# A hybrid attention and state-space layer: every float32r tile at multiples of 64 bytes, a set order around the first LayerNorm and the first FFN block, and LayerNorm's scale in the transposes' eviction

## The chip, the cores and the metric

The kernel runs on one core of a Trainium2 chip. Its time is the device time of one execution, in microseconds (us). Before the change the median of three runs is 1178.77 us (1176.41 to 1178.85).

## The reference

One decoder layer for 512 tokens of width 1024, all in float32. A combined projection gives the queries, keys, values and forget gates of an attention part, the z, x, B, C and dt of a Mamba-2 part, and two branch gates. Both branches are projected to 1024 columns, merged by the gates and projected once more. Two LayerNorms and a SwiGLU FFN with 2816 hidden columns follow:

```
proj = x @ w_in
q, k, v, f_logit, z, xbc, dt_raw, gate_logit = split(proj)
attn_d = forgetting_attention(q, k, v, log_sigmoid(f_logit + b_forget)) @ w_proj_attn
ssm_d  = mamba2_branch(z, xbc, dt_raw, ...) @ w_proj_ssm
gates  = sigmoid(gate_logit + b_gates)
mixed  = (gates[0] * attn_d + gates[1] * ssm_d) @ w_out
x = layer_norm(alpha * x + mixed, ln1_g, ln1_b)
h = (silu(x @ w_ffn_gate) * (x @ w_ffn_up)) @ w_ffn_down
x = layer_norm(alpha * x + h, ln2_g, ln2_b)
```

## The kernel before

**Products.** Each float32 GEMM is three matmuls of float32r operands (`mm3`, L113 to L116). Both operands are split (L79 to L81): `hi` is a cast on ScalarE (ACT), `lo` the rest, a subtraction on VectorE (DVE). The three are hi times hi, hi times lo and lo times hi. TensorE holds 128x128 of the one operand (stationary, the second name in a profile row) and streams the columns of the other (moving, the first name), 512 or 256 at a time. Weights come from DRAM in tiles of 128x1024 (`raw`), 512 KB a load on SyncE's queue (SP), and are split under high priority into `whi` and `wlo` (three buffers each).

**Order of the work.** Projections with the scan, in four groups; attention; the branch gates and the merge (up to 757 us); the output projection; the first LayerNorm; six column blocks of the FFN; the down projection with the second LayerNorm. A scheduler puts each engine's instructions in an order; where nothing has priority that is nearly the order of the code.

**The output projection** (`gemm_down`, L151) runs in four quarters: two pairs of 128-token tiles (`th_`) by two column halves, 48 matmuls of 512 columns each. `evac_res` (L684 to L687) adds the residual and takes the statistics of a half row. `layer_norm` (L689 to L699) joins them into `mv`, takes the root on GpSimd (POOL, L693), and applies mean, gain, root and bias in two DVE instructions of 1024 columns, with gain and bias spread over all partitions in `t_gz`. The result goes to DRAM as `x1_d` (L728), and in 16 transposes for each token pair (L733) to PSUM. From there ACT copies it to `xf` (L739), and for tokens 0 and 1 a split makes the FFN operands B11 and B21 (L738).

**The FFN** computes each GEMM of 512 hidden columns (256 in the last block) with seven products of quarters, in this order of passes: P1, P2, P6, P5, P7, P3, P4. A pass is 24 matmuls of 256 columns (12 in the last block). The token operands are B11, B21, NT2, NT1, T3, B22 and T4 (`x_operands`, made all at once). The weight operands are quarters or sums of quarters: a11, a12, a11 + s1, s1, s3, a12 + a11, a22. s1 and s3 are sums of two quarters, made by a load on SP and an adding load on POOL (L787, L789); the other sums are DVE's (L807, L812). Their splits stand under high priority (L792 to L798). A block b has a gate GEMM (Gb in this text, PSUM banks `gps`) and an up GEMM (Ub, banks `cps`). Banks are emptied by a copy, a sum, and SwiGLU's two steps (L830, L833, L877 to L881). Block 0 runs two passes of G0 and of U0, then the operands, then the rest.

**The down projection** takes `h`, split again, against 22 weight chunks of 24 matmuls of 512 columns, 528 in all. The residual comes back from `x1_d` (L915), and the second LayerNorm stands at the end.

**Places in SBUF.** Pools place tiles one behind another, from the left or right end. In the programs as built the float32r operands begin at these bytes, modulo 128:

| | before | after |
| --- | --- | --- |
| xh, xl, t_uh, t_ul, t_xtok, t_gz, t_bT, t_cT, t_btok, t_cbm, t_xst, t_xdt, t_v, t_th | 64 | 64 |
| whi, wlo (stream of weights), t_ab, t_nw, t_hn | 96 | 64 |
| FFN tokens b11, b21 | 96 | 64 |
| FFN tokens nt1, nt2, t3, t4, b22, down projection ht | 32 | 64 |
| FFN weights wh, wl: two of the four buffers / the other two | 96 / 32 | 64 / 64 |

Of the kernel before, what the change touches and what calls it, by code (L numbers as in the profile page):

```python
# [37 lines left out]
def tile_hybrid_decoder_layer(  # L38
# [681 lines left out]
    xop = {"B11": operand(bop, "b11"), "B21": operand(bop, "b21")}  # L720
    for th_ in range(2):
        tts = (2 * th_, 2 * th_ + 1)
        for half in ((1, 0), (0, 1))[th_]:
            gemm_down(wo_chunk, KD, tok(mx), tts, half, evac_res, gps)
        for tt in tts:
            for _ in layer_norm(tt, gb):
                pass
            nc.gpsimd.dma_start(out=x1_d[tt], in_=xr[tt])  # L728
            for i in range(2):
                ps = cps()  # L730
                for k in range(4):
                    kt = 4 * i + k
                    nc.tensor.transpose(out=ps[:, k * P:(k + 1) * P], in_=xr[tt][:, kt * P:(kt + 1) * P], identity=ident)  # L733
                ps = ps.rearrange("p (k t) -> p k t", k=4)
                ts = slice(tt * P, (tt + 1) * P)
                if th_ == 0:
                    hi, lo = xop[("B11", "B21")[i]]
                    split(hi[:, :, ts], lo[:, :, ts], ps)  # L738
                nc.scalar.copy(out=xf[i][:, :, ts], in_=ps)  # L739

    left1.close()
    hb = pool(ctx, "hb", "left")
    tp = pool(ctx, "tp", "left")
    top = pool(left2, "top", "left")
    wops.append(pool(left2, "wop1", "left"))
    nops = [0]
    tmp2 = pool(left2, "tmp2", "left")

    def t_tile(dtype=F32):
        return tp.tile([P, 1024], dtype, name="T", bufs=4)

    def x_operands():
        B = {(k, t): xf[k - 1][:, :, (t - 1) * 256:t * 256] for k in (1, 2) for t in (1, 2)}

        def new(nm, make):
            t = t_tile().rearrange("p (k t) -> p k t", k=4)
            make(t)
            xop[nm] = operand(top, nm.lower())  # L760
            split(*xop[nm], t)
            return t
        v = nc.vector
        nt1 = t_tile().rearrange("p (k t) -> p k t", k=4)
        v.tensor_tensor(out=nt1, in0=B[1, 1], in1=B[1, 2], op=ALU.subtract)
        nt2 = new("NT2", lambda t: v.scalar_tensor_tensor(out=t, in0=nt1, scalar=-1.0, in1=B[2, 2], op0=ALU.mult, op1=ALU.subtract))
        xop["NT1"] = operand(top, "nt1")
        split(*xop["NT1"], nt1)
        new("T3", lambda t: v.tensor_tensor(out=t, in0=B[2, 2], in1=B[1, 2], op=ALU.subtract))
        xop["B22"] = operand(top, "b22")  # L770
        split(*xop["B22"], B[2, 2])
        new("T4", lambda t: v.scalar_tensor_tensor(out=t, in0=nt2, scalar=-1.0, in1=B[2, 1], op0=ALU.mult, op1=ALU.subtract))
# [44 lines left out]
    PASSES = (("X", "B11"), ("Y", "B21"), ("X", "NT2"), ("Z", "NT1"), ("X", "T3"), ("Z", "B22"), ("X", "T4"))

    def ffn_gemm(w, c0, F, alloc, quadrant):


        nj = F // P
        n = nj * 256
        ops = quarters(w, c0, F)
        bank = {}
        cp = {}

        def keep(nm, src):
            cp[nm] = tmp2.tile([P, T], F32, name="cp", bufs=4)[:, 0:n]
            nc.scalar.copy(out=cp[nm], in_=src)  # L830

        def add(nm, src):
            nc.vector.tensor_tensor(out=cp[nm], in0=src, in1=cp[nm], op=ALU.add)  # L833
            return cp[nm]

        for i, (b, x_) in enumerate(PASSES):
# [128 lines left out]
```

## Time and profile before

| | us |
| --- | --- |
| median of three runs | 1178.77 (1176.41 to 1178.85) |
| profiled execution | 1178.42 |
| its span | 1176.7 |
| TensorE busy in the span | 1138.1 |
| VectorE busy | 770.5 |
| ScalarE busy | 525.6 |
| GpSimd busy | 135.6 |

The mean granted TensorE clock is 0.988 of full speed. The profile has five engines: PE (matmuls), PEld (PE's weight loads, beside its matmuls), DVE, ACT and POOL, and SP for loads. A row out<-in gives the tile written and the tiles read, "x" a count. For a matmul the names behind the arrow are moving, stationary.

### The profile page before, as it was taken

How to read it: one execution, taken by the hardware profiler on the slowest of the kernel's cores; microseconds unless marked ns; L12 is line 12 of the kernel's file. 1: busy time of each engine (PE TensorE's matmuls, PEld its weight loads, DVE VectorE, ACT ScalarE, POOL GpSimd, SP SyncE). 2: the span in 40 equal slices, each digit the busy share in tenths (PEclk: the TensorE clock that was granted, in tenths of full speed). 3: DMA queues.
4: the chain of work that ended last, by engine and by line, in shares of the span. 5: the costliest groups of instructions: out<-in, count | busy, mean ns of one | idle time of the engine just before them, and what ended most of it. 6: DMA issues, size and time to landing. Idle time of an engine off the chain costs nothing.

```text
span 1176.7 us, 15773 instructions
## 1 busy us (share of the span) xinstructions
PE 1138.1 (97%) x6086; PEld 947.5 (81%) x6086; DVE 770.5 (65%) x1210; ACT 525.6 (45%) x906; POOL 135.6 (12%) x165
## 2 busy tenths in 40 slices
PE   7999999999999999999999999989799999999997
PEld 5787877778777788777777888877799999988885
DVE  3579964883885654887788344556787777764326
ACT  3376773453441423665566353213454544453120
POOL 2003131030231100211110000021001111100001
PEclk8999999999999999999999999989899999999999
DMA  8343243243231233121211355372577877473311
GB/s 241 91 129 125 73 126 90 78 116 95 90 91 55 89 90 93 52 73 55 73 55 55 90 161 161 119 203 79 118 199 176 201 179 171 94 252 97 103 54 72
DMA packets 115707, 134.20 MB, mean 114 GB/s; under 512 B 5588, under 2 KB 93872, under 8 KB 115504
## 3 DMA queue, kind: packets, MB, share of 16 engines
q1 hardware_dynamic: 99328, 112.80, 31.4%
q0 software_dynamic: 14576, 14.09, 7.6%
q10 hardware_dynamic: 1728, 6.29, 1.5%
q8 instruction: 48, 0.79, 0.3%
q14 instruction: 27, 0.22, 0.1%
HBM read 128.77 MB, written 4.26 MB: 113 GB/s over the span
## 4 chain that ended last, share of the span: by engine, by line
PE 45%; DVE 3%; issue 3%; DMA 1%; ACT 1%; POOL 1%; SPq 0%; DVEq 0%; POOLq 0%; ACTq 0%
PE gps L114 9%; PE gps L116 9%; PE gps L115 9%; PE cps L116 5%; PE cps L115 5%; PE cps L114 5%; DMA rq<-in_w_ffn_up_dram 1%; PE cps L433 1%; PE cps L427 1%; DVE xr L698 0%; DVE wl L81 0%; POOL mv L693 0%; PE cps L405 0%; DVE t_sd L698 0%; DMA t_sd<-in_x_dram 0%
## 5 line engine op out<-in xcount | busy, mean ns | idle before, releaser
L81 DVE TENSOR_TENSOR wlo<-raw,whi 128x1024 fp32r<-128x1024 f32 x127 | 156.2, 1230 | 226.5 <-ACT whi L80 226.2
L80 ACT CAST whi<-raw 128x1024 fp32r<-128x1024 f32 x127 | 132.9, 1047 | 279.4 <-PE gps L116 113.1
L114 PE MATMUL gps<-xh,whi 128*128 128x512 f32 x456 | 183.2, 402 | 0.0
L115 PE MATMUL gps<-xl,whi 128*128 128x512 f32 x456 | 183.0, 401 | 0.0
L116 PE MATMUL gps<-xh,wlo 128*128 128x512 f32 x456 | 182.9, 401 | 0.0
L80 ACT CAST wh<-rq 128x1024 fp32r<-128x1024 f32 (+1 forms) x84 | 81.9, 978 | 123.8 <-PE cps L115 46.6
L81 DVE TENSOR_TENSOR wl<-rq,wh 128x1024 fp32r<-128x1024 f32 (+1 forms) x84 | 94.9, 1133 | 42.3 <-ACT wh L80 42.1
L115 PEld LDWEIGHTS gps<-xl,whi 128*128 128x128 f32 x456 | 86.0, 189 | 18.0 <-issue 0.2
L114 PEld LDWEIGHTS gps<-xh,whi 128*128 128x128 f32 x456 | 85.9, 188 | 18.1 <-issue 0.2
L116 PEld LDWEIGHTS gps<-xh,wlo 128*128 128x128 f32 x456 | 86.0, 189 | 17.2
L114 PE MATMUL gps<-whi,xh 128*128 128x512 f32 x192 | 77.4, 404 | 3.8 <-ACT xh L80 3.8
L115 PE MATMUL gps<-wlo,xh 128*128 128x512 f32 x192 | 77.1, 402 | 0.0
L116 PE MATMUL gps<-whi,xl 128*128 128x512 f32 x192 | 77.1, 402 | 0.0
L212 DVE SCALAR_TENSOR_TENSOR t_v<-gps,cw,t_v 128x511 f32<-128x511 f32 (+2 forms) x72 | 53.5, 745 | 4.4 <-ACT t_v L209 3.6
L116 PE MATMUL gps<-t_uh,wlo 128*128 128x512 f32 x128 | 51.7, 404 | 0.0
L115 PE MATMUL gps<-t_ul,whi 128*128 128x512 f32 x128 | 51.6, 403 | 0.0
L114 PE MATMUL gps<-t_uh,whi 128*128 128x512 f32 x128 | 51.2, 400 | 0.0
L114 PEld LDWEIGHTS gps<-whi,xh 128*128 128x128 f32 x192 | 36.6, 191 | 13.6 <-ACT xh L80 4.5
L789 POOL DMA_DIRECT2D rq<-in_w_ffn_gate_dram x12 | 15.5, 1294 | 265.9 <-PE gps L116 168.8
L412 ACT ACTIVATE t_y<-t_y,sm 128x128 f32<-128x128 f32 (+1 forms) x64 | 35.7, 559 | 19.4 <-DVE sm L410 17.7
L115 PEld LDWEIGHTS gps<-wlo,xh 128*128 128x128 f32 x192 | 36.7, 191 | 9.2 <-DVE wlo L81 0.5
L116 PEld LDWEIGHTS gps<-whi,xl 128*128 128x128 f32 x192 | 36.5, 190 | 9.1 <-DVE xl L81 0.3
(562 smaller groups left out, 2782.1 us busy)
## 6 DMA issues: line engine op xcount, KB each, us to landing
raw<-in_w_in_dram SPq DMA_DIRECT2D x80, 512.0 KB, 3.7
rq<-in_w_ffn_gate_dram SPq DMA_DIRECT2D x25, 512.0 KB, 6.1
rq<-in_w_ffn_up_dram SPq DMA_DIRECT2D x25, 512.0 KB, 4.9
raw<-in_w_ffn_down_dram SPq DMA_DIRECT2D x22, 512.0 KB, 3.7
t_ab<-ac_d SPq DMA_DIRECT2D x32, 256.0 KB, 3.4
raw<-in_w_proj_ssm_dram SPq DMA_DIRECT2D x16, 512.0 KB, 3.5
rq<-in_w_ffn_gate_dram POOLq DMA_DIRECT2D x10, 512.0 KB, 6.9
rq<-in_w_ffn_up_dram POOLq DMA_DIRECT2D x10, 512.0 KB, 6.0
```

Of the source, the lines that this page charges most:

```text
L80: nc.scalar.copy(out=hi, in_=src)
L81: nc.vector.tensor_tensor(out=lo, in0=src, in1=hi.bitcast(F32), op=ALU.subtract)
L114: nc.tensor.matmul(out=o, lhsT=l[0], rhs=r[0], start=start, stop=False, skip_group_check=skip)
L115: nc.tensor.matmul(out=o, lhsT=l[0], rhs=r[1], start=False, stop=False, skip_group_check=skip)
L116: nc.tensor.matmul(out=o, lhsT=l[1], rhs=r[0], start=False, stop=stop, skip_group_check=skip)
L212: nc.vector.scalar_tensor_tensor(out=v[:, sh:], in0=ps[:, 0:T - sh], scalar=cw[:, k, blk:blk + 1], in1=v[:, sh:], op0=ALU.mult, op1=ALU.add)
L412: nc.scalar.activation(out=pt[:, 0:n], in_=pt[:, 0:n], func=AF.Exp, scale=-1.0, bias=sm[:, 2:3], accum_out=sm[:, 0:1])
L427: nc.tensor.transpose(out=ps[:, o:o + P], in_=pr[i][:, kb * P:(kb + 1) * P], identity=ident)
L433: nc.tensor.matmul(out=po[:, kb * P:], lhsT=vt[:, kb, hh, :], rhs=pT[kb][j], start=kb == 0 and j == 0, stop=kb == NT - 1 and j == 1)
L789: nc.gpsimd.dma_start(out=v(t), in_=s_, accum_op=ALU.add)
```

## The change

1. **Places.** A tile of 32 bytes a partition ahead of the right pools (`pad`) and one in `hb` (`pad2`); `lnv` takes 64 bytes of `cst0`, and `mv` has two buffers for four. The table above has what follows.
2. **LayerNorm.** The first one only normalises: one DVE instruction of 1024 columns, (x - mean) * root. ln1's gain and bias are loaded as 16 more rows of a transpose at the start (`lnv`), and stand as scale and bias in ACT's eviction of each transpose, 128 columns apiece, in place of one copy of 512. `x1_d` holds the normalised rows; behind the reload before the down projection, eight DVE instructions apply gain and bias to them.
3. **Order.** A class `Gemm` takes the place of the generators: loads, operands, multiply and evacuate are written out for block 0; from there on an operand is made two passes ahead, without priority, and loads stand at fixed passes. `rq` slots are fixed by tag, and `cp` has five buffers for four.

```diff
+    pool(ctx, "pad", "right").tile([P, 8], F32, name="pad")
...
+    lnv = cst0.tile([P, 16], F32, name="lnv")
...
-    vrs = carve(P, parts=40)
-    for r0, src in ((0, conv_b), (24, b_gates)):
+    vrs = carve(P, parts=56)
+    for r0, src in ((0, conv_b), (24, b_gates), (40, ln1_g), (48, ln1_b)):
...
+    nc.vector.tensor_copy(out=lnv, in_=ps[:, 136:152])
...
-    gb = load_gb(slot("gz", (P, 2, D)), ln1_g, ln1_b)
...
+            for nm in names:
+                if self.slots:
+                    i = self.slots[nm]
+                else:
+                    i, rq_order[0] = rq_order[0], (rq_order[0] + 1) % 8
+                t = self.raw[nm] = rqp.tile([P, 1024], F32, name="rq", tag=f"rq{i}", bufs=1)[:, 0:4 * self.F]
+                nc.sync.dma_start(out=self.v(t), in_=self.q(*src[nm][0]))
+                for s_ in src[nm][1:]:
+                    nc.gpsimd.dma_start(out=self.v(t), in_=self.q(*s_), accum_op=ALU.add)
...
-            with tc.high_priority():
-                split(*o, t)
-            return [v(i) for i in o]
...
+            split(*o, t)
+            self.ops[p_] = [self.v(i) for i in o]
...
+    def normalise(tt):
+        mv = moments(tt)
+        nc.vector.tensor_scalar(out=xr[tt], in0=xr[tt], scalar1=mv[:, 0:1], scalar2=mv[:, 2:3], op0=ALU.subtract, op1=ALU.mult)
...
+            for k in range(4):
+                kt = 4 * i + k
+                nc.scalar.activation(out=xf[i][:, k, tt * P:(tt + 1) * P], in_=ps[:, k * P:(k + 1) * P], func=AF.Identity,
+                                     scale=lnv[:, kt:kt + 1], bias=lnv[:, 8 + kt:9 + kt])
+        nc.gpsimd.dma_start(out=x1_d[tt], in_=xr[tt])
...
+    G0.load("a11", "a12", "s1", "s3", "a22")
+    U0.load("a11", "a12", "s1")
+    wo_half(0, 1)
+    wo_half(0, 0)
+    for tt in (0, 1):
+        normalise(tt)
+    G0.op("P1")
+    G0.op("P2")
+    wo_half(1, 0)
+    for tt in (0, 1):
+        x1_transposed(tt)
...
+    wo_half(1, 1)
+    for tt in (2, 3):
+        normalise(tt)
+    G0.multiply("P1")
+    G0.multiply("P2")
+    for tt in (2, 3):
+        x1_transposed(tt)
...
+    hb.tile([P, 8], F32, name="pad2")
...
+    U0.op("P1")
+    U0.op("P2")
+    U0.run("P1")
+    nt1 = x_operand("NT1", lambda t: vec_.tensor_tensor(out=t, in0=B[1, 1], in1=B[1, 2], op=ALU.subtract))
+    G0.op("P5")
+    U0.run("P2")
...
+    AHEAD = 2
+    for i, (g_, p_) in enumerate(rest):
+        if p_ == "P7" and i + 3 < len(rest):
+            rest[i + 3][0].load("a11", "a12", "s1")
+        if p_ == "P4" and i + 1 < len(rest):
+            rest[i + 1][0].load("s3", "a22")
...
+        if i + AHEAD < len(rest):
+            rest[i + AHEAD][0].op(rest[i + AHEAD][1])
+        g_.run(p_)
...
+    for op_, src in ((ALU.mult, ln1_g), (ALU.add, ln1_b)):
+        t = end.tile([P, D], F32, name="gb1")
+        nc.scalar.dma_start(out=t, in_=src.partition_broadcast(P))
+        for tt in range(NT):
+            nc.vector.tensor_tensor(out=xr[tt], in0=xr[tt], in1=t, op=op_)
+    gb = load_gb(end.tile([P, 2, D], F32, name="gb2"), ln2_g, ln2_b)
```

**PE at the end of the output projection's third quarter, before.** The transposes of tokens 0 and 1 (L733) begin inside the quarter, four products ahead of its end; t_cbm, t_xdt, t_btok and t_xst hold w_out, xh and xl the merged tokens.

```order
L114 MATMUL gps<-t_cbm,xh_6047 128x512
L115 MATMUL gps<-t_xdt,xh_6047 128x512
L116 MATMUL gps<-t_cbm,xl_6049 128x512
L114 MATMUL gps<-t_btok,xh_6047 128x512
L733 MATMUL cps<-ident,t_sd 128x128 x8
L115 MATMUL gps<-t_xst,xh_6047 128x512
```

**The same place now.** All 16 transposes (now L855; `mm3` is L116 to L118) stand together behind the quarter, and the fourth quarter, on t_xtok, behind them.

```order
L116 MATMUL gps<-t_cbm,xh_6056 128x512
L117 MATMUL gps<-t_xdt,xh_6056 128x512
L118 MATMUL gps<-t_cbm,xl_6058 128x512
L855 MATMUL cps<-ident,t_sd 128x128 x16
L116 MATMUL gps<-t_xtok,xh_6055 128x512
L117 MATMUL gps<-t_xtok,xh_6055 128x512
```

The transposes moved from inside the quarter to the border of two quarters.

**DVE between the first LayerNorm and the FFN operand NT1, before.** L81 is the lower half of a split, L807 and L812 are sums of weight quarters, L833 and L878 empty banks, L765 and L766 make NT1 and NT2.

```order
L833 TENSOR_TENSOR cp<-gps,cp 128x512
L81 TENSOR_TENSOR wl<-rq,wh 128x1024 x3
L807 TENSOR_TENSOR rq<-rq 128x1024
L878 SCALAR_TENSOR_TENSOR g<-g,cp 128x512
L812 TENSOR_TENSOR rq<-rq 128x1024
L81 TENSOR_TENSOR wl<-rq,wh 128x1024
L765 TENSOR_TENSOR T<-xf 128x1024
L833 TENSOR_TENSOR cp<-cps,cp 128x512
L81 TENSOR_TENSOR wl<-rq,wh 128x1024
L881 SCALAR_TENSOR_TENSOR h<-g,cp 128x2x256
L766 SCALAR_TENSOR_TENSOR T<-T,xf 128x1024
L81 TENSOR_TENSOR nt1l<-T,nt1h 128x1024
```

**The same place now.** L83 is the lower half of a split, L848 the normalisation, L766 and L768 the weight sums, L781 and L831 empty banks, L909 and L912 make NT1 and NT2.

```order
L695 TENSOR_SCALAR mv<-mv 128x1
L83 TENSOR_TENSOR wl<-rq,wh 128x1024
L848 TENSOR_SCALAR t_sd<-t_sd,mv 128x1024
L781 TENSOR_TENSOR cp<-gps,cp 128x512
L83 TENSOR_TENSOR wl<-rq,wh 128x1024
L766 TENSOR_TENSOR rq<-rq 128x1024
L768 TENSOR_TENSOR rq<-rq 128x1024
L909 TENSOR_TENSOR T<-xf 128x1024
L912 SCALAR_TENSOR_TENSOR T<-T,xf 128x1024
L831 SCALAR_TENSOR_TENSOR g<-g,cp 128x512
L781 TENSOR_TENSOR cp<-cps,cp 128x512
L83 TENSOR_TENSOR nt1l<-T,nt1h 128x1024
```

One split, one bank sum and U0's first product step (L881) that stood ahead of NT1's lower half now stand elsewhere; splits of weights stand between the LayerNorm's small instructions.

## Rows read from the trace of the kernel before

**Rows 1.** The page, busy time of each engine in the span.

```profile
PE 1138.1 (97%) x6086; PEld 947.5 (81%) x6086; DVE 770.5 (65%) x1210; ACT 525.6 (45%) x906; POOL 135.6 (12%) x165
```

**Rows 2.** Stages: us, busy PE, PEld, DVE, ACT, POOL, clock, DMA share, GB/s.

```profile
500.00:650.00 150.00, 148.92 (x743) 115.50 (x742) 122.29 (x323) 90.64 (x203) 16.56 (x32) 1.00 0.23 64
650.00:757.00 107.00, 107.00 (x463) 86.74 (x462) 46.65 (x54) 38.34 (x49) 0.00 (x0) 1.00 0.39 120
757.24:866.17 108.93, 95.45 (x561) 85.43 (x560) 70.91 (x85) 34.75 (x46) 16.81 (x15) 0.92 0.58 151
866.17:1024.19 158.02, 158.02 (x1347) 158.02 (x1345) 120.81 (x132) 79.90 (x98) 20.56 (x16) 1.00 0.73 170
1046.11:1155.50 109.39, 109.39 (x470) 88.17 (x469) 40.26 (x38) 29.52 (x29) 0.00 (x0) 1.00 0.34 116
```

**Rows 3.** Waits of PE in 750 to 870 us: total us, times, longest.

```profile
PE cps L733 <- DVE mv L692: 3.2, 1, 3.2
PE gps L114 <- ACT nt2h L80: 3.0, 1, 3.0
```

**Rows 4.** Two parts of the stage at 757 us, columns as in rows 2.

```profile
783.11:808.66 25.55, 22.40 (x95) 18.42 (x94) 12.01 (x18) 4.50 (x8) 3.49 (x4) 0.87 0.13 46
825.49:866.17 40.68, 33.25 (x243) 32.43 (x242) 30.00 (x31) 17.87 (x21) 3.84 (x3) 0.87 0.57 139
```

**Rows 5.** Timeline of PE, matmuls of 512 columns: start us, duration us.

```profile
649.05 0.39 PE L115 MATMUL gps<-xl,whi 128*128 128x512 f32 x1
...
713.21 0.39 PE L114 MATMUL gps<-t_hn,whi 128*128 128x512 f32 x1
...
722.19 0.40 PE L114 MATMUL gps<-t_ab,whi 128*128 128x512 f32 x1
...
726.27 0.40 PE L114 MATMUL gps<-t_gz,whi 128*128 128x512 f32 x1
...
757.24 0.39 PE L114 MATMUL gps<-t_xtok,xh 128*128 128x512 f32 x1
...
783.11 0.39 PE L114 MATMUL gps<-t_btok,xh 128*128 128x512 f32 x1
```

**Rows 6.** Timeline of PE, matmuls of 256 columns and the successor of one.

```profile
476.05 0.28 PE L406 MATMUL cps<-t_cT,t_xdt 128*128 128x256 f32 x1
476.17 0.34 PE L405 MATMUL cps<-t_bT,t_xst 68*128 68x384 f32 x1
...
854.86 0.28 PE L116 MATMUL cps<-nt2h,wl 128*128 128x256 f32 x1
...
860.61 0.28 PE L116 MATMUL cps<-t3h,wl 128*128 128x256 f32 x1
...
866.06 0.28 PE L116 MATMUL cps<-t4h,wl 128*128 128x256 f32 x1
```

**Rows 7.** Groups by line, PE: count, busy us, mean ns of one, idle before.

```profile
L114 PE MATMUL gps<-xh,whi 128*128 128x512 f32 x456 | 183.2, 402 | 0.0
L114 PE MATMUL gps<-whi,xh 128*128 128x512 f32 x192 | 77.4, 404 | 3.8 <-ACT xh L80 3.8
L114 PE MATMUL gps<-t_uh,whi 128*128 128x512 f32 x128 | 51.2, 400 | 0.0
```

**Rows 8.** Groups by line and form, DVE and ACT.

```profile
L81 DVE TENSOR_TENSOR wl<-rq,wh 128x1024 fp32r<-128x1024 f32 x70 | 85.3, 1222 | 38.7 <-ACT wh L80 38.7
L686 DVE SCALAR_TENSOR_TENSOR t_sd<-t_sd,gps 128x512 f32<-128x512 f32 x8 | 5.5, 682 | 10.0 <-PE gps L116 10.0
L414 DVE TENSOR_SCALAR t_y<-t_y,sm 128x512 f32<-128x512 f32 x16 | 7.8, 485 | 0.4
L294 ACT ACTIVATE t_ab<-t_ab,acum 128x128 f32<-128x128 f32 x128 | 41.4, 390 | 4.7 <-DMA t_ab<-ac_d 4.4 <-PE cps L300 0.2
```

**Rows 9.** The page, DMA issues: count, KB each, median us to landing.

```profile
rq<-in_w_ffn_gate_dram SPq DMA_DIRECT2D x25, 512.0 KB, 6.1
rq<-in_w_ffn_gate_dram POOLq DMA_DIRECT2D x10, 512.0 KB, 6.9
```

More of the change, by code (lines that the diff above doesn't have):

```diff
@@ L715, in tile_hybrid_decoder_layer @@
     xf = [h_tile(4).rearrange("p (k t) -> p k t", k=4) for _ in range(2)]
+    B = {(k, t): xf[k - 1][:, :, (t - 1) * 256:t * 256] for k in (1, 2) for t in (1, 2)}
     def operand(p_, nm):
         return [p_.tile([P, 4, 256], F32R, name=nm + i) for i in "hl"]
[L720 to L739, printed above, removed]
@@ L743, in tile_hybrid_decoder_layer @@
[L743 to L772, printed above, removed]
@@ L817, in tile_hybrid_decoder_layer @@
[L817 to L836, printed above, removed]
-            first = b not in bank
+    rq_order = [0]
@@ L883, in up @@
                                            in1=o.rearrange("p (j t) -> p j t", j=nj), op0=ALU.mult, op1=ALU.mult)
-        return ffn_gemm(w_fg, b * 512, F, gps, gate), ffn_gemm(w_fu, b * 512, F, cps, up)
-    for b in range(6):
-        gate, up = ffn_block(b)
-        if b == 0:
-            for gen in (gate, up):
-                for _ in range(2):
-                    next(gen)
-            x_operands()
-        for gen in (gate, up):
-            for _ in gen:
-                pass
+        return Gemm(w_fg, b * 512, F, gps, gate, slots[0]), Gemm(w_fu, b * 512, F, cps, up, slots[1])
@@ new lines, in tile_hybrid_decoder_layer @@
+    G0, U0 = ffn_block(0, (dict(a11=0, a12=1, s1=2, s3=3, a22=4), dict(a11=5, a12=6, s1=7, s3=2, a22=7)))
+    G0.load("a11", "a12", "s1", "s3", "a22")
[9 more added lines that the diff above has]
+        x1_transposed(tt)
+    xop = {}
+    for nm, k in (("B11", 1), ("B21", 2)):
+        xop[nm] = operand(bop, nm.lower())
+        split(*xop[nm], B[k, 1])
@@ new lines, in tile_hybrid_decoder_layer, with t_tile, x_operand @@
+    wo_half(1, 1)
[5 more added lines that the diff above has]
+        x1_transposed(tt)
+    left1.close()
+    hb = pool(ctx, "hb", "left")
+    hb.tile([P, 8], F32, name="pad2")
+    tp = pool(ctx, "tp", "left")
+    top = pool(left2, "top", "left")
+    wops.append(pool(left2, "wop1", "left"))
+    tmp2 = pool(left2, "tmp2", "left")
+    def t_tile(dtype=F32):
+        return tp.tile([P, 1024], dtype, name="T", bufs=4)
+    def x_operand(nm, make):
+        t = t_tile().rearrange("p (k t) -> p k t", k=4)
+        make(t)
+        xop[nm] = operand(top, nm.lower())
+        split(*xop[nm], t)
+        return t
@@ new lines, in tile_hybrid_decoder_layer @@
+    G0.evacuate("P1")
+    G0.evacuate("P2")
+    vec_ = nc.vector
+    U0.op("P1")
[4 more added lines that the diff above has]
+    U0.run("P2")
+    nt2 = x_operand("NT2", lambda t: vec_.scalar_tensor_tensor(out=t, in0=nt1, scalar=-1.0, in1=B[2, 2], op0=ALU.mult, op1=ALU.subtract))
+    U0.op("P5")
+    G0.run("P5")
+    U0.load("s3")
+    G0.op("P6")
+    U0.run("P5")
+    U0.load("a22")
@@ new lines, in tile_hybrid_decoder_layer @@
+    U0.op("P6")
+    x_operand("T3", lambda t: vec_.tensor_tensor(out=t, in0=B[2, 2], in1=B[1, 2], op=ALU.subtract))
+    G0.run("P6")
+    G0.op("P7")
+    U0.run("P6")
+    xop["B22"] = operand(top, "b22")
+    split(*xop["B22"], B[2, 2])
+    G0.op("P3")
+    G0.run("P7")
+    x_operand("T4", lambda t: vec_.scalar_tensor_tensor(out=t, in0=nt2, scalar=-1.0, in1=B[2, 1], op0=ALU.mult, op1=ALU.subtract))
+    G0.op("P4")
+    G0.run("P3")
+    U0.op("P7")
+    G0.run("P4")
+    rest = [(U0, p_) for p_ in ("P7", "P3", "P4")]
@@ new lines, in tile_hybrid_decoder_layer @@
+    for b in range(1, 6):
+        for g_ in ffn_block(b):
+            rest += [(g_, p_) for p_ in ("P1", "P2", "P6", "P5", "P7", "P3", "P4")]
+    AHEAD = 2
[4 more added lines that the diff above has]
+            rest[i + 1][0].load("s3", "a22")
+        if i == 0:
+            for k in range(1, AHEAD):
+                rest[k][0].op(rest[k][1])
+        if i + AHEAD < len(rest):
+            rest[i + AHEAD][0].op(rest[i + AHEAD][1])
+        g_.run(p_)
```

129 lines of the change are left out of this document (73 added, 56 removed).

## The prediction

> **What bounds the kernel now.** I read the engine line of the page, then busy times by stage, then TensorE's waits, then single matmuls in order of time. TensorE (PE in the rows) is busy 97% of the span [rows 1]. By stage [rows 2] it never stops in the gate and attention-merge stage (107.0 of 107.0 us), in FFN blocks 1 to 4 (158.02 of 158.02) and in the down projection (109.39 of 109.39). One stage is different: from the first matmul of the output projection (757.24) to the first of FFN block 1 (866.17) it is busy 95.45 of 108.93 us, so 13.5 us idle. [...] Two things therefore set the time: how far apart matmuls start where PE never stops, and what is lost in this one stage.
>
> A matmul's own duration (0.40 us) overlaps the next, so the spacing has to be taken from starts [rows 5]. From 649.05 to 713.21 lie 275 matmuls of 512 columns: 233.3 ns each. From 757.24 to 783.11 lie 114 of the same size: 226.9. From 722.19 to 726.27 lie 18: 227. What differs is where operands begin, by the table of starts in the section on the kernel. In the slow run the moving operand (xh, xl) begins at 64 modulo 128 and the stationary one that is loaded behind it (whi, wlo) at 96; in the fast runs both begin at 64, or both at 96. In the down projection they are at 96 and 32, and 109.39 us for 469 matmuls [rows 2] give 233.2. So for 512 columns equal remainders are fast, whatever they are. For 256 columns it is the other way [rows 6]: 48 matmuls with both at 32 take 5.75 us, 119.8 ns each; the next 48, at 32 and 96, take 5.45 us, 113.5 ns each. The one 256-column kind with both at 64, at 476.05, is 0.12 us from its successor.
>
> **The change part by part. Placement.** In the program as built after the change every float32r operand begins at 64 modulo 128: all pairs become equal. For 512 columns that is 233.3 to 227.0, 6.3 ns each. The groups are 456, 192 and 128 matmuls on each of three lines [rows 7], 2,328 in all, with 576 more by the code (48 of the merge on t_gz, 528 of the down projection): 2,904 x 6.3 = 18.3 us at most. Some are followed by a transpose or a scan matmul instead, and in the attention stage DVE is busy 122.29 of 150 us [rows 2] and may become the limit. I take four fifths, 14.5 us; bounds 7 (the stages with scan and attention return nothing) and 18.3. For 256 columns there are 1,848 matmuls (five blocks of 336 and one of 168). Blocks 1 to 4 start 1,344 in 158.02 us, 117.6 ns each; with equal remainders 119.8: 1,848 x 2.2 = 4.1 us lost. Bounds: 113.5 ns would give 7.6 us instead, 120.0 would cost 4.4. I take the loss, since both equal kinds (32 and 96) and the one at 64 agree.
>
> **The stage at 757.** PE's work is the same set, in another order. The transposes of tokens 0 and 1 now stand behind the whole third quarter of the output projection (48 matmuls, 10.9 us), so the LayerNorm on DVE and POOL is over when PE comes to them: the 3.2 us for mv [rows 3] go. Call E the end of the projection. PE then has two passes of G0 (48 matmuls, 5.8 us), 16 transposes, and two passes of U0 (5.8 us) before it needs NT1. DVE's order between the projection's last sums and NT1's lower half is: four half-size instructions of the residual and its statistics at 0.68 us [rows 8], two normalisations (one TENSOR_SCALAR of 1024 columns each; 512 take 0.485 us, so below 0.97), four splits, two weight sums, NT1, NT2 and NT1's lower half at 1.22 us (nine, 11.0 us), two bank sums and one gate at 0.68, and small ones of the moments: 2.7 + 1.9 + 11.0 + 2.0 + 0.7 = 18.3 us, begun 1.3 us before E, since the first token tile ends early. So NT1 is whole at about E+17. PE has 13.3 us of work till then, so 3.7 us of idle remain: some behind tokens 2's transposes, the rest before NT1. ACT's 16 evictions of 128 columns with scale and bias (below 0.39 us each, the row of the same kind from SBUF [rows 8]; 6.2 us together) end at about E+13, ahead of DVE, and hide. Behind NT1 each further operand comes from a DVE that needs 1.2 to 3.7 us per pass pair of 5.8 us, so no more waits. Idle goes from 13.5 to 3.7 us: 9.8 won. Half clock: 0.13 of 25.55 and of 40.68 us [rows 4], 8.6 us lost before. Every fall there follows idle of the kind that goes; I leave 1.5 us, bounds 0 and 4.3 (half of it stays): 7.1 won. Together 16.8; bounds 8 (as much new waiting as half of what went) and 18.4.
>
> **At nothing.** Gain and bias return as eight DVE instructions of 1.22 us, 9.8 us, in the down projection, where DVE is busy 40.26 of 109.39 us [rows 2]; without that cover they would cost all of it. ACT's queue there holds the second of their loads until four of them are done, and the weight casts stand behind it; a chunk is 24 matmuls, 5.4 us, and the casts run up to three chunks ahead, against 6.1 us for a load of that size [rows 9]. The two small loads and 16 more rows of one transpose at the start I put at nothing, since no engine but POOL issues them; 0 to 2 us. The tail behind the last matmul is unchanged.
>
> **Sum.** The profiled execution took 1178.4 us, 0.4 below the median shown. 1178.4 - 14.5 + 4.1 - 16.8 = 1151.2.
>
> **Rivals.** (1) Placement changes nothing, and what I took for it is the stage's. Time 1178.4 - 16.8 = 1161.6. For it: the pairs differ in tiles and stage too. Against it: with the same whi and wlo (96), t_ab and t_nw (96) step at 227 ns where xh and xl (64) stepped at 233 [rows 5]. Chance 0.08. [...] (2) The stage returns half: the splits no longer have priority over the evictions, the lower halves come late pass by pass, and a new fall of the clock follows. 1178.4 - 14.5 + 4.1 - 8 = 1160. For it: DVE is the chain there; against it: each split stands two passes ahead in the new order. Chance 0.15. (3) 256-column matmuls at 64 go to 113.5: 1178.4 - 14.5 - 7.6 - 16.8 = 1139.5. Against it stand all equal rows. Chance 0.06. (4) Slower. The sum s1 of two weight quarters comes by a load on SP and an adding one on POOL, 6.1 and 6.9 us [rows 9]. It is now asked for at pass P7 of the GEMM before, five passes or 14.4 us ahead of its use in P6, and in SP's new order s1 of G1 stands behind four other quarters. DVE waits for it in order, with the lower halves behind it. Later than 14.4 us, each further microsecond is lost once in each of 11 GEMMs: 4 us late give 1151 + 44 = 1195. It decides from 14.4 us on, which is only 1.4 above 13.0; against it: the slots are free well before, and DMA is at 0.73 in those blocks with no PE idle [rows 2]. Chance 0.05.
>
> **Numbers.** The forecast has 0.66 and its own range of 1145 to 1157. The range 1141 to 1166 takes in rivals 1 and 2 and leaves out 3, 4 and the ends. A measurement of this kernel tells some 0.2% from no change (2.4 us). Faster by more 0.94, within 0.01, slower 0.05, which is rival 4.
>
> **What would show it.** Starts of 512-column matmuls at 227 ns in every stage, the down projection near 106.5 us; FFN blocks 1 to 4 near 161 us, slower than now; the stage at 757 some 92 us, with one gap of two to three microseconds before NT1 and little at half clock; no wait of PE in the down projection. I am wrong if the 512-column spacing stays at 233, if the FFN blocks get faster, or if DVE waits for a DMA in each of their GEMMs.

## The result and the profile after

The changed kernel takes 1158.78 us (median of four runs, 1158.32 to 1159.27), the kernel before 1178.26 beside it: a ratio of 0.9837, 95% interval 0.9820 to 0.9854. The forecast was 1151.2, in a range of 1141 to 1166. The span fell from 1176.7 to 1157.3 us, 19.4 us where 27.2 were forecast.

The page's engine line for the kernel after, beside [rows 1]:

```profile
PE 1125.0 (97%) x6086; PEld 946.7 (82%) x6086; DVE 772.4 (67%) x1213; ACT 532.2 (46%) x928; POOL 135.3 (12%) x167
```

Stages of the kernel after, columns as in [rows 2]; the output projection begins at 748.14, the FFN's first pass at 793.43, block 1 at 845.50, the down projection at 1025.75 (their windows are set some 0.06 us later):

```profile
650.00:748.20 98.20, 98.20 (x435) 81.32 (x434) 43.73 (x50) 36.41 (x46) 0.00 (x0) 1.00 0.40 124
748.20:845.56 97.36, 91.00 (x562) 82.73 (x561) 64.28 (x79) 41.15 (x68) 15.44 (x15) 0.96 0.64 162
748.20:793.49 45.29, 45.29 (x210) 37.74 (x209) 21.46 (x31) 12.32 (x24) 6.32 (x7) 1.00 0.60 163
793.49:845.56 52.07, 45.71 (x354) 45.00 (x353) 42.82 (x49) 28.82 (x44) 9.13 (x8) 0.93 0.66 162
845.56:1005.82 160.26, 160.26 (x1346) 160.26 (x1346) 120.86 (x131) 80.31 (x98) 20.55 (x16) 1.00 0.70 167
1025.80:1148.50 122.70, 122.70 (x529) 99.18 (x528) 62.48 (x71) 28.39 (x28) 2.77 (x3) 1.00 0.36 119
```

The same 275 matmuls of 512 columns that took 233.3 ns each in [rows 5]:

```profile
642.25 0.39 PE L117 MATMUL gps<-xl,whi 128*128 128x512 f32 x1
...
704.62 0.39 PE L116 MATMUL gps<-t_hn,whi 128*128 128x512 f32 x1
```

62.37 us by 275 are 226.8 ns. PE has no idle time left in the output projection: 45.29 of 45.29 us. What is left lies behind it, 6.36 us in 793 to 846, at a clock of 0.93. Blocks 1 to 4 take 160.26 us against 158.02, longer, as forecast. The down projection takes 122.70; its steps are 232.4 ns, which is 109.0 us for the 469 of [rows 2], where 106.5 was named as the sign. So it did not go to 227, though all its operands now begin at 64 modulo 128. That is the first reading that the prediction has no room for.

Waits of PE from 740 to 850 us in the kernel after, beside [rows 3]:

```profile
PE cps L116 <- DVE cp L781: 3.6, 1, 3.6
PE gps L117 <- DVE nt1l L83: 1.8, 1, 1.8
PE cps L855 <- DVE t_sd L848: 1.0, 1, 1.0
```

The two lower ones are the 3.7 us forecast (2.8 measured). The upper one is new: U0's last pass waits for a bank that DVE should have emptied. DVE itself waits. Its waits from 820 to 845 us, and pieces of the chain that ended last, in order of time:

```profile
DVE rq L766 <- DMA rq<-in_w_ffn_gate_dram: 4.5, 1, 4.5
```

```profile
811.88 0.21 PE gps L117
...
831.98 7.01 DMA rq<-in_w_ffn_gate_dram
839.18 1.05 issue
840.23 0.69 DVE cp L781
...
841.77 0.21 PE cps L117
```

The adding load of G1's s1 is issued at 831.98 and lands 7.01 us later. DVE has the sum a11 + s1 (L766) in its queue ahead of the bank's emptying, and stands for 4.5 us. Behind this idle, and behind the one before NT1, matmuls of 256 columns step at 0.21 us, where 0.12 is usual [rows 6]: the granted clock is 0.93 in the stretch, and 0.50 from 812 to 813 and from 842 to 843 us, as it is 0.50 from 831.5 to 836 us in the kernel before.

By stage, for this and for all whole kernels that follow, in us (from the starts of matmuls in their profiled executions; the last stage ends with the start of the last matmul), and the ratio of each to the kernel before that ran beside it:

| | to output projection | to block 1 | blocks 1 to 4 | block 5 | down projection | median | ratio (95%) |
| --- | --- | --- | --- | --- | --- | --- | --- |
| before | 757.2 | 108.9 | 158.0 | 19.8 | 124.0 | 1178.3 | |
| place_only | 748.8 | 108.9 | 160.3 | 20.0 | 123.9 | 1172.85 | 0.9954 (0.9941 to 0.9967) |
| order_only | 755.3 | 97.6 | 157.7 | 19.8 | 123.2 | 1166.24 | 0.9899 (0.9877 to 0.9921) |
| after | 748.1 | 97.4 | 160.3 | 20.0 | 122.7 | 1158.78 | 0.9837 (0.9820 to 0.9854) |
| s1_slot | 748.5 | 90.5 | 160.3 | 20.0 | 122.7 | 1152.42 | 0.9781 (0.9764 to 0.9799) |
| ln_dve | 748.2 | 90.6 | 160.3 | 20.0 | 123.4 | 1154.42 | 0.9792 (0.9777 to 0.9806) |
| tokens_192 | 748.3 | 90.7 | 161.3 | 20.2 | 119.7 | 1151.45 | 0.9768 (0.9752 to 0.9784) |
| ffn_192 | 748.0 | 90.2 | 159.2 | 19.9 | 120.4 | 1148.69 | 0.9741 (0.9727 to 0.9756) |
| ffn_all | 748.8 | 90.1 | 158.3 | 19.8 | 119.8 | 1147.48 | 0.9729 (0.9691 to 0.9767) |
| ffn_alt | 748.9 | 89.7 | 152.3 | 19.0 | 119.8 | 1140.52 | 0.9673 (0.9651 to 0.9695) |

### The profile page after: what moved, and what is told of

It reads as the page before. It is cut to its first block, busy times and chain, and to the rows that moved or that the text cites. A ratio compares the mean times of both kernels' runs of the same rounds, so it can differ in the third digit from the quotient of the medians.

```text
span 1157.3 us, 15804 instructions
## 1 busy us (share of the span) xinstructions
PE 1125.0 (97%) x6086; PEld 946.7 (82%) x6086; DVE 772.4 (67%) x1213; ACT 532.2 (46%) x928; POOL 135.3 (12%) x167
## 4 chain that ended last, share of the span: by engine, by line
PE 49%; DVE 2%; ACT 1%; DMA 1%; issue 0%; DVEq 0%; ACTq 0%
PE gps L116 11%; PE gps L117 11%; PE gps L118 11%; PE cps L117 5%; PE cps L116 5%; PE cps L118 5%; PE cps L429 1%; PE cps L435 1%; DMA rq<-in_w_ffn_gate_dram 1%; ACT xf L858 0%; DVE xr L705 0%; PE cps L407 0%; PE cps L408 0%; DVE xr L704 0%; DVE st L690 0%
## 5 line engine op out<-in xcount | busy, mean ns | idle before, releaser
L83 DVE TENSOR_TENSOR wlo<-raw,whi 128x1024 fp32r<-128x1024 f32 x127 | 156.1, 1230 | 209.7 <-ACT whi L82 209.2
L116 PE MATMUL gps<-xh,whi 128*128 128x512 f32 x456 | 181.3, 398 | 0.0
L118 PE MATMUL gps<-xh,wlo 128*128 128x512 f32 x456 | 180.9, 397 | 0.0
L83 DVE TENSOR_TENSOR wl<-rq,wh 128x1024 fp32r<-128x1024 f32 (+1 forms) x84 | 95.0, 1132 | 38.3 <-ACT wh L82 38.2
L116 PEld LDWEIGHTS gps<-xh,whi 128*128 128x128 f32 x456 | 85.9, 188 | 16.4 <-issue 0.2
L118 PEld LDWEIGHTS gps<-xh,wlo 128*128 128x128 f32 x456 | 86.0, 188 | 15.5
L116 PE MATMUL gps<-whi,xh 128*128 128x512 f32 x192 | 75.9, 396 | 3.4 <-ACT xh L82 3.4
L118 PE MATMUL gps<-whi,xl 128*128 128x512 f32 x192 | 76.1, 396 | 0.0
L118 PE MATMUL gps<-t_uh,wlo 128*128 128x512 f32 x128 | 51.0, 399 | 0.0
L116 PE MATMUL gps<-t_uh,whi 128*128 128x512 f32 x128 | 50.5, 394 | 0.0
L116 PEld LDWEIGHTS gps<-whi,xh 128*128 128x128 f32 x192 | 36.6, 191 | 12.1 <-ACT xh L82 4.1
L296 ACT ACTIVATE t_ab<-t_ab,acum 128x128 f32<-128x128 f32 x128 | 41.4, 390 | 5.8 <-DMA t_ab<-ac_d 3.9
```

What stands on the lines that cost most here:

```text
L83: nc.vector.tensor_tensor(out=lo, in0=src, in1=hi.bitcast(F32), op=ALU.subtract)
L116: nc.tensor.matmul(out=o, lhsT=l[0], rhs=r[0], start=start, stop=False, skip_group_check=skip)
L118: nc.tensor.matmul(out=o, lhsT=l[1], rhs=r[0], start=False, stop=stop, skip_group_check=skip)
L296: nc.scalar.activation(out=m[:, r, :], in_=m[:, r, :], func=AF.Relu, scale=-1.0, bias=acum[:, c, h:h + 1])
```

## Experiments

Below, distance is the start of the stationary operand of the next matmul less the start of the moving one, in bytes modulo 256. Within a group or a pass all stationary starts are the same modulo 256, so no run here tells the next matmul's stationary operand from its own.

**place_only: the two pads alone, on the kernel before.**

```diff
+    pool(ctx, "pad", "right").tile([P, 8], F32, name="pad")
     left1, right1 = ExitStack(), ExitStack()
...
     hb = pool(ctx, "hb", "left")
+    hb.tile([P, 8], F32, name="pad2")
```

> The kernel before with the two pads alone: all starts as after, order and LayerNorm as before. Theory A: output projection from 757.2 to about 748.2 us, blocks 1 to 4 from 158.0 to 160.3, down projection from 123.9 to 122.7, the stage between as before: 1178.3 - 9.0 + 2.5 - 1.2 = 1170.5 us. Theory C: no change, 1178.3, and the gain before 748 us belongs to something else.

1172.85 us. Windows of place_only: the stage from the output projection to block 1, blocks 1 to 4, the down projection:

```profile
748.95:857.83 108.88, 94.88 (x562) 84.97 (x562) 71.25 (x85) 34.71 (x46) 16.81 (x15) 0.94 0.58 151
857.83:1018.10 160.27, 160.27 (x1346) 160.27 (x1346) 120.54 (x132) 79.77 (x99) 20.56 (x16) 1.00 0.72 168
1038.08:1162.02 123.94, 123.30 (x528) 98.66 (x527) 54.24 (x63) 30.26 (x30) 2.77 (x3) 1.00 0.34 116
```

Pads that no instruction touches move the time: 8.5 us less up to the output projection (the 275 matmuls of [rows 5] step at 226.7 ns), 2.2 more in blocks 1 to 4, nothing in between. Rival 1 of the prediction falls. The total stays 2.4 us above the 1170.5 of theory A, and the down projection gets nothing, where 1.2 us were expected: its steps are 233.3 ns, as before, though every operand in it begins where it does in the kernel after, whose steps are 232.4. So the starts alone do not fix this spacing. The short wait of 0.6 us at the head of the stage is not the reason either, since ln_dve below has the same wait and steps at 232.4. It is left open.

**order_only: the kernel after without the two pads.**

```diff
-    pool(ctx, "pad", "right").tile([P, 8], F32, name="pad")
...
-    hb.tile([P, 8], F32, name="pad2")
```

> The kernel after without the two pads: order and LayerNorm as after, all starts as before. Theory A: the stage from the output projection to block 1 shrinks from 108.9 to about 97.4 us and nothing else moves: 1178.3 - 11.5 = 1166.8 us. If order and places help each other, the sum of both single parts misses the whole 19.5 us by more than 1 us. Theory C: 1159, as after.

1166.24 us. The same stage, and blocks 1 to 4:

```profile
755.35:852.96 97.61, 90.47 (x562) 82.06 (x561) 64.14 (x79) 41.14 (x68) 15.44 (x15) 0.97 0.65 162
852.96:1010.61 157.65, 157.65 (x1346) 157.65 (x1346) 120.79 (x131) 80.40 (x98) 20.57 (x16) 1.00 0.72 169
```

The stage is as short as after, the FFN as fast as before. The ratios give 0.46% for the places and 1.01% for the order with the new LayerNorm, 1.47% together; the whole change has 1.63%, within the intervals. The two parts act on different stages and add up.

**s1_slot: the buffers of G1's s1 and s3 exchanged, on the kernel after.** In the kernel after s1 of G1 takes the buffer in which U0's s3 lies until its split ends at 826 us, and stands last of G1's loads in SP's queue. Exchanged, it takes one that is free from 817 us on. (The edit exchanges the two buffers for whatever later GEMMs put there, too.)

```diff
-                    i, rq_order[0] = rq_order[0], (rq_order[0] + 1) % 8
+                    i, rq_order[0] = (0, 1, 3, 2, 4, 5, 6, 7)[rq_order[0]], (rq_order[0] + 1) % 8
```

> The kernel after with the buffers of G1's s1 and s3 exchanged, so that s1 no longer waits for U0's s3 to be split. Theory D (the 3.9 us of PE's idle at 837 us, and the low clock behind it, come from DVE waiting for s1's adding load): DVE's wait of 4.5 us goes, PE's idle goes, and with the low clock behind it 4 to 6 us: 1153 to 1155 us. Rival (the buffer is not what holds it, or the next late operand takes its place): within 1 us of 1158.8.

1152.42 us, 6.4 below the kernel after and 0.6 below the range that was expected. The stage of s1_slot, and PE's waits from 735 to 850 us:

```profile
748.50:839.01 90.51, 87.74 (x561) 79.63 (x560) 63.72 (x79) 41.21 (x68) 15.45 (x15) 1.00 0.67 171
```

```profile
PE gps L117 <- DVE nt1l L83: 1.7, 1, 1.7
PE cps L855 <- DVE t_sd L848: 1.0, 1, 1.0
```

The wait of 3.6 us is gone and no other took its place, and DVE waits for no load from 820 to 845 us: the buffer, and the place in SP's queue that goes with it, was the cause. The stage gets 6.9 us shorter, idle time being only 3.6 of it; most of the rest is the clock, 1.00 for 0.96. Of that rest 1.6 us stood behind the wait that is gone. Another 1.4 is not explained: after the unchanged wait for NT1 some 18 steps were 0.21 us in the kernel after, and all but 3 are 0.12 here. Why the same idle stretch is followed by a lower clock in one kernel and not in the other is left open.

**ln_dve: LayerNorm as before, in the new order, on s1_slot.** Not in the lines below: gain and bias are loaded into `t_gz` again, and the eight DVE instructions before the second LayerNorm go.

```diff
-        nc.vector.tensor_scalar(out=xr[tt], in0=xr[tt], scalar1=mv[:, 0:1], scalar2=mv[:, 2:3], op0=ALU.subtract, op1=ALU.mult)
+        nc.vector.scalar_tensor_tensor(out=xr[tt], in0=xr[tt], scalar=mv[:, 0:1], in1=gb1[:, 0, :], op0=ALU.subtract, op1=ALU.mult)
+        nc.vector.scalar_tensor_tensor(out=xr[tt], in0=xr[tt], scalar=mv[:, 2:3], in1=gb1[:, 1, :], op0=ALU.mult, op1=ALU.add)
...
-                nc.scalar.activation(out=xf[i][:, k, tt * P:(tt + 1) * P], in_=ps[:, k * P:(k + 1) * P], func=AF.Identity,
-                                     scale=lnv[:, kt:kt + 1], bias=lnv[:, 8 + kt:9 + kt])
+            nc.scalar.copy(out=xf[i][:, :, tt * P:(tt + 1) * P], in_=ps.rearrange("p (k t) -> p k t", k=4))
```

> s1_slot with the first LayerNorm as before the change: gain and bias in two DVE instructions of 1024 columns from t_gz, plain copies of 512 columns behind the transposes, no gain and bias at the end; the order stays. DVE gets 1.6 us more for each token tile, ACT 3.2 us less for each pair of tiles. By the prediction (ACT's evictions hide behind DVE): NT1 comes 3.3 us later, 1155 to 1157 us. Rival (the evictions, 5.6 us in the chain of waits of the kernel after, are themselves what NT1 waits for): what DVE loses ACT gives back, within 1 us of 1152.4.

The stage is the same, 90.61 for 90.51 us:

```profile
748.30:838.91 90.61, 87.59 (x563) 79.60 (x562) 69.58 (x83) 33.91 (x45) 14.98 (x15) 1.00 0.68 177
```

DVE has 5.9 us more in it and ACT 7.3 less. For the stage the rival held: what the new LayerNorm takes from DVE it puts on ACT, and NT1's lower half ends no earlier by it (810.5 us in s1_slot, 809.7 in ln_dve). In this order it is worth nothing there. The median, 1154.42 us, lies between the two expectations, 2.0 us above s1_slot; the ratios differ by 0.0011, within their intervals, so a difference is not shown. The profile has 0.7 us of it in the down projection, 0.6 of them the wait of PE at its head.

**offsets: spacing against distance, by itself.** All matmuls of a group read the same two operands in one tile; the loop of the sweep is this (comment added):

```
for N in (512, 256):
    for mov in (0, 96):
        for d in range(0, 512, 32):
            group(N, mov, mov + d)      # 32 matmuls, moving at mov, stationary at mov + d
```

> Leaves out the whole layer: only matmuls of float32r operands on otherwise idle engines, 32 in a row for each pair of starts, 512 and 256 columns. The moving operand begins at 0 or 96 bytes, the stationary one at 0 to 480 bytes behind it, in steps of 32. Theory A (the spacing depends on the distance of the two starts, modulo 256): 512 columns 227 ns at distances 0 and 256, 232 to 234 at all others, among them 128 and 384; 256 columns 119.9 at 0 and 256, 118.6 at 128, 113 to 115 at 192 and 448, 117 at 64 and 320; the same for both moving starts. Theory B (modulo 128, as in the prediction, and the down projection is slow for another reason): 227 also at 128 and 384, and 120 for 256 columns there. Theory C (places do nothing, the stage decides): one spacing for all distances.

Timeline of PE, groups of 512 columns, dac at 32 bytes and each next one 32 further; a group's spacing is the start of the next less its own, by 32:

```profile
38.06 7.62 PE L67 MATMUL dac<-op 128*128 128x512 f32 x32
45.52 7.63 PE L67 MATMUL dad<-op 128*128 128x512 f32 x32
...
60.47 7.59 PE L67 MATMUL daf<-op 128*128 128x512 f32 x32
67.90 7.63 PE L67 MATMUL dag<-op 128*128 128x512 f32 x32
75.37 7.49 PE L67 MATMUL dah<-op 128*128 128x512 f32 x32
82.70 7.63 PE L67 MATMUL dai<-op 128*128 128x512 f32 x32
90.16 7.42 PE L67 MATMUL daj<-op 128*128 128x512 f32 x32
97.42 7.62 PE L67 MATMUL dak<-op 128*128 128x512 f32 x32
```

At 32 bytes (dac) 7.46 us by 32 are 233 ns; at 128 (daf) 232; at 192 (dah) 229; at 256 (daj) 227, as at 0. The second half of the sweep repeats the first, and so does the one with the moving operand at 96. So the period is 256 bytes: 128 is not a good distance, and that is the one of the down projection in the kernel after (moving at 192, stationary at 64 modulo 256). Theory A holds for 512 columns but for the 229 at 192; B and C fall. For 256 columns A's numbers fail: the mean is 119.5 at 0, 117.8 at 64 and at 192, 120.1 at 128, flatter than the kernel's rows, 113 nowhere.

**tokens_192: the left pad 128 bytes longer, on s1_slot.**

```diff
-    hb.tile([P, 8], F32, name="pad2")
+    hb.tile([P, 40], F32, name="pad2")
```

> s1_slot with the one pad in front of the left tiles 128 bytes longer (160 for 32): FFN tokens, second half of the weights, and the down projection's tokens begin at 192 modulo 256, like everything else, so every distance is 0 modulo 256. Theory A: down projection from 122.7 to 120 us (527 matmuls from 232.4 to 227), blocks 1 to 4 from 160.3 to 161.1 (119.25 to 119.9): 1152.4 - 2.8 + 1.1 = 1150.7 us. Theory B (modulo 128 decides, the down projection is slow for another reason): no change, 1152.4.

Blocks 1 to 4 and the down projection of tokens_192:

```profile
839.03:1000.31 161.28, 161.28 (x1346) 161.28 (x1345) 120.99 (x132) 80.17 (x98) 20.56 (x16) 1.00 0.72 167
1020.47:1140.22 119.75, 119.75 (x529) 98.76 (x527) 62.10 (x70) 28.41 (x28) 2.77 (x3) 1.00 0.37 121
```

As forecast: 119.75 us are 227 ns for each step of the down projection, 3.0 us won, and 1.0 lost in the FFN, where all distances are now 0 and the step is 120.0.

**offsets_ffn: the FFN's pattern by itself.** Groups of 48, with hi and lo tiles and row blocks as in a pass (the loop, shortened):

```
for r in range(2):
    for js in range(2):
        for k in range(4):
            for u, v in ((0, 0), (0, 1), (1, 0)):
                matmul(lhsT=wo[u][:, k, js * 128:(js + 1) * 128], rhs=xo[v][:, k, :])
```

> Leaves out the whole layer: matmuls in the FFN's own pattern (hi, hi, lo of the weights by hi, lo, hi of the tokens, four row blocks, two column blocks, 48 in a row) on otherwise idle engines. Three placings of tokens and weights: both low in SBUF, tokens low and weights high, tokens high and weights low; distances 0, 8, 16, 32 and on by 32 to 224 bytes. The plain rows gave 117.8 ns at 192 and 64; in the kernel before, 192 stood at 114.8 and 64 at 117.2. Theory A1 (the pattern of alternating tiles makes the difference): about 114 at 192 in all three placings. Theory A2 (it is the place of the tiles, low or high): 114 in one placing only. Theory A3 (it is the kernel's other engines): 117.8 in all. For 512 columns with this pattern: 227 at 0, 233 elsewhere.

Timeline of PE, both operands low: dae at 32 bytes, daf 64, dag 96, dah 128, dai 160, daj 192, dak 224:

```profile
40.05 5.84 PE L80 MATMUL dae<-low 128*128 128x256 f32 x48
45.73 5.61 PE L80 MATMUL daf<-low 128*128 128x256 f32 x48
51.17 5.93 PE L80 MATMUL dag<-low 128*128 128x256 f32 x48
56.94 5.85 PE L80 MATMUL dah<-low 128*128 128x256 f32 x48
62.63 5.91 PE L80 MATMUL dai<-low 128*128 128x256 f32 x48
68.38 5.81 PE L80 MATMUL daj<-low 128*128 128x256 f32 x48
74.03 5.83 PE L80 MATMUL dak<-low 128*128 128x256 f32 x48
```

By 48, 64 bytes (daf) give 113.3 ns and 192 (daj) 117.7; the two other placings give the same. A2 and A3 fall. For 512 columns the pattern gives 227.6 at 0, 229.0 at 192, 232.5 at 128 and 233.2 to 234.1 elsewhere, as in offsets. A1 is half right: 113 is there, but at 64, while in the kernel before it stood at 192 [rows 6]. Distance alone does not decide.

**ffn_192: five of seven FFN operands at distance 192, on s1_slot.**

```diff
-    hb.tile([P, 8], F32, name="pad2")
+    hb.tile([P, 56], F32, name="pad2")
...
+    pool(left2, "padl", "left").tile([P, 48], F32, name="pad3")
     wops.append(pool(left2, "wop1", "left"))
...
     htp = pool(ctx, "htp", "left")
+    htp.tile([P, 48], F32, name="pad4")
```

> s1_slot with other pads: five of the seven FFN token operands begin at 0 modulo 256 and all weights at 192, distance 192; B11 and B21 stay at distance 0; the down projection's tokens at distance 0, but for those of block 0. 1,320 FFN matmuls from 119.25 to 114.3 if the kernel before is the measure (6.5 us), to 117.8 if the plain rows are (1.9); 528 at 119.9 (0.3 lost); 432 of the down projection from 232.4 to 227 (2.4 won). 1152.4 - 8.6 = 1143.8 us, or 1148.4. Theory B: no change, 1152.4.

1148.69 us, the smaller of the two gains: in blocks 1 to 5 every pass at distance 192 steps at 117.8 ns, none at 113.

**history: how a spacing is entered.** Groups as in offsets_ffn, with weights high.

> Leaves out the whole layer: the FFN's pattern of 256 columns again, 48 in a row, six times a group at distance 0 followed by three groups at 64 or 192 bytes, entered in different ways: the stationary operand 64 higher or lower, the moving one 64 higher or lower, both moved. Theory H (at distances 64 and 192 there are two steady spacings, 113.4 and 117.8 ns; which one is set on entry and then kept): the groups entered by a start 64 lower run at 113.4, those by a start 64 higher at 117.8, and the two groups behind each keep that, whatever their distance. Rival (the distance alone decides, 64 at 113.4 and 192 at 117.7 as in the row of distances, and what the kernel before showed against it comes from its other engines): each group by its own distance, no memory.

Timeline of PE. dab is distance 0. Then, as (start of moving, of stationary, both against dab): dac (0, +64), dad (0, -64), dae (0, +64), daf (0, 0), dag (0, -64), dah (0, +64), dai (0, -64), daj (0, 0), dak (+64, 0):

```profile
23.57 5.79 PE L80 MATMUL dab<-low,high 128*128 128x256 f32 x47
29.20 5.82 PE L80 MATMUL dac<-low,high 128*128 128x256 f32 x48
34.86 5.81 PE L80 MATMUL dad<-low,high 128*128 128x256 f32 x48
40.51 5.60 PE L80 MATMUL dae<-low,high 128*128 128x256 f32 x48
45.95 5.92 PE L80 MATMUL daf<-low,high 128*128 128x256 f32 x48
51.71 5.60 PE L80 MATMUL dag<-low,high 128*128 128x256 f32 x48
57.15 5.60 PE L80 MATMUL dah<-low,high 128*128 128x256 f32 x48
62.59 5.60 PE L80 MATMUL dai<-low,high 128*128 128x256 f32 x48
68.03 5.92 PE L80 MATMUL daj<-low,high 128*128 128x256 f32 x48
73.79 5.82 PE L80 MATMUL dak<-low,high 128*128 128x256 f32 x48
```

dac and dah have the same operands at the same places: 5.66 us for 48 the first time, 5.44 the second, 117.9 and 113.3 ns. dad and dag likewise. The rival falls: at 64 and 192 there are two spacings. From distance 0, a start 64 lower led to 113.3 (dag), one 64 higher to 117.8 (dac, dak), and 113.3 was then kept. Theory H missed one thing: 117.8 is not kept for ever; the stationary start going up by 128 bytes (dad to dae) turned it into 113.3. The groups behind dak that stay at 64 and 192 agree: dal, entered by the same step of 128 up, has 113.3, and a moving start 64 lower, from distance 0, leads to 113.7 and then 113.3. The kernel before has both spacings too, by the starts of the program as built: at distance 192, T4 of block 1's gate GEMM, entered from distance 0 by a stationary start 64 lower, steps at 113.3, and NT2 of the same GEMM, behind passes at 117.8, at 117.9. It also shows that 113.3 can be lost: from the last pass of block 0 (113.3) to the first of block 1 the moving start goes 64 lower and the stationary one 64 higher, and the spacing is 117.9.

**ffn_all: all weights at distance 192 from the third pass on, on s1_slot.** Tokens stay at 192 modulo 256, weights go to 128.

```diff
-    wops = [pool(right2, "wop0", "right")]
+    first = ExitStack()
+    wops = [pool(first, "wop0", "right")]
...
     left1.close()
+    first.close()
+    pool(right2, "padw", "right").tile([P, 16], F32, name="pad3")
+    wops[0] = pool(right2, "wopb", "right")
     hb = pool(ctx, "hb", "left")
-    hb.tile([P, 8], F32, name="pad2")
+    hb.tile([P, 40], F32, name="pad2")
...
+    pool(left2, "padl", "left").tile([P, 48], F32, name="pad4")
     wops.append(pool(left2, "wop1", "left"))
```

> s1_slot with all FFN tokens at 192 and all weights at 128 modulo 256 but for the first two passes (the weights' first buffers are given up behind them and taken again 64 bytes lower), and the down projection's tokens at 192, distance 0. Theory H: entered by a start 64 lower, all passes from the third on at 113.4 ns: blocks 1 to 4 from 160.3 to 152.4 us, block 5 and block 0 1.5 us less, down projection 2.9 less: 1152.4 - 12.3 = 1140 us. Rival (distance 192 is 117.8 ns): blocks 1 to 4 158.3, 1152.4 - 2.0 - 0.4 - 2.9 = 1147 us.

1147.48 us: the rival's number, 117.8 ns from the third pass to the last. Between the two passes at distance 0 and the third stand 16 transposes and a wait, so the entry is not the one of history.

**ffn_alt: distances 64 and 192 in turn, on ffn_all.** One pad of 64 bytes in place of 192 puts the second half of the weights at 0 modulo 256, so that the stationary start changes by 128 modulo 256 every two passes.

```diff
-    pool(left2, "padl", "left").tile([P, 48], F32, name="pad4")
+    pool(left2, "padl", "left").tile([P, 16], F32, name="pad4")
```

> ffn_all with the second half of the weights at 0 instead of 128 modulo 256 (one pad of 64 for 192 bytes), same instructions in the same order: the weights now change between distance 64 and distance 192 every two passes. In history such a change upward by 128 bytes took the slow steady spacing (117.8) to the fast one (113.3), and a change in either direction kept the fast one. Theory H: some passes at 117.8 at the start, then 113.4 to the end of block 5: blocks 1 to 4 from 158.3 to 152.4 us, block 5 from 19.7 to 19.1, 1147.5 - 7 to 8 = 1140 us. Rival (in the kernel the other engines or the transposes settle it at 117.8): no change, 1147.5.

1140.52 us, 0.9673 of before (0.9651 to 0.9695), below both kernels. Blocks 1 to 4 of ffn_all, then of ffn_alt:

```profile
838.90:997.19 158.29, 158.29 (x1346) 158.29 (x1346) 121.54 (x133) 80.29 (x98) 20.56 (x16) 1.00 0.74 172
```

```profile
838.60:990.92 152.32, 152.32 (x1346) 152.32 (x1346) 120.99 (x133) 79.96 (x98) 20.56 (x16) 1.00 0.77 180
```

All instructions and their order are the same in both; 6.0 us lie between them. Passes 3 to 10 still step at 117.8 ns, all later ones at 113.3. Three such changes went by before the fourth turned it, so a change may set it and need not.

## Why the prediction was right, and where its terms were off

The sign, the stages and most of the mechanism held; the sum was 27.2 us and 19.4 came.

- **The number.** The parts measured 9.1 us up to the output projection, 11.6 in the stage behind it and 1.2 in the down projection, less 2.4 lost in the FFN's blocks: 19.5. 1158.78 us lies outside the forecast's own 1145 to 1157 and inside the range of 1141 to 1166, which was made to take in rivals 1 and 2. Rival 1 did not happen, and rival 2 not as described, so part of the hit is the width of the range.
- **512 columns, 14.5 us.** Measured 8.5 (place_only) to 9.1 up to the output projection. In the down projection the spacing gave 0.5 us (233.3 to 232.4 ns); the rest of its 1.2 is a wait of 0.6 us and what hung on it, which order_only loses too. The step that failed is "So for 512 columns equal remainders are fast, whatever they are", with remainders taken modulo 128, and with it "all pairs become equal". The period is 256, and there the down projection's pairs stand 128 apart. Of the 14.5 us 2.7 were its own (four fifths of 528 x 6.3 ns). Elsewhere the spacing came nearly as forecast, 227.7 ns on average over some 2,400 steps for 227.0, but the stages with scan and attention gave less back than four fifths.
- **256 columns, 4.1 us lost.** 2.2 in blocks 1 to 4 and 0.2 in block 5. The sign held. The size was off since half of the pairs stand at distance 128 and step at 118.6 ns, not at 119.8.
- **The stage at 757, 16.8 us.** 11.6: PE's idle is 6.4 us for the 3.7 forecast, and the steps at half clock cost about 3.0 for the 1.5 left. The wait for mv is gone, the idle up to NT1 came out at 2.8 us for 3.7, and NT1's lower half ended 16.7 us behind the projection's end, for 17 forecast. What failed is "Behind NT1 each further operand comes from a DVE that needs 1.2 to 3.7 us per pass pair of 5.8 us, so no more waits". It counts DVE's work and not its wait for a load, which rival 4 had: s1's adding load, late behind other quarters in SP's queue. It struck in G1 alone, for 3.6 us of PE's idle and 1.6 at the lower clock behind it (18 steps of 0.21 for 0.12 us), and not in 11 GEMMs: G1's s1 had been given a buffer that U0's s3 held to 826 us, and from block 1 to the down projection DVE waits for no load and PE has no idle. With that buffer exchanged (s1_slot) the stage is 18.4 us shorter than before, the upper bound of this term.
- **At nothing.** The eight DVE instructions at the end are hidden: DVE is busy 62.48 of 122.70 us in the down projection and PE has no idle there. ACT's 16 evictions took 5.7 us together where 6.2 was the bound (one lasts 0.49 us and not below 0.39, but they overlap), and did not hold DVE up; but ln_dve shows that the stage is as short without them.
- **Rivals.** 1 fell by place_only. 2 named 8 us for the stage, it was 11.6; a new fall of the clock came, but behind one late load and not from lower halves late pass by pass. 3 was wrong for this change, whose distances are 0 and 128, and right that 113.3 is to be had: ffn_alt has it.

## What to carry to other kernels

Where PE never stops, take the spacing from starts, by size and by the places of both operands: one number in a pad's shape was worth 7 us here (ffn_all to ffn_alt), the hand-written order with its LayerNorm 12 (order_only). For float32r matmuls like these, distance 0 modulo 256 was best for 512 columns, and 64 or 192 for 256 columns (113.3 or 117.8 ns, against 120.0 at 0). Look at the whole period before writing an alignment rule. When an order is written by hand, follow each sum's load back through its queue and its buffer: the engine that waits may be two steps from the one that idles.

## What had not been expected of the hardware

The start-to-start time of float32r matmuls depends on the distance between the moving and the stationary operand with a period of 256 bytes: for 512 columns 226.7 ns at 0, 229 at 192, 232 at 128 and 233 to 234 at the other multiples of 32. At 128 the kernels show two values for the same starts, 232.4 ns in the kernel after and 233.3 in place_only. For 256 columns at distances 64 and 192 the same instructions on the same places step at 113.3 or at 117.8 ns, and keep to one for hundreds of matmuls (113.3 from the 11th pass of ffn_alt to the last). What sets it was only narrowed down: the history of starts ahead of it, on idle engines too. Why is open.
